# Stage one's value projection by seven block products, opened with the products that need no input sums

## The chip, the cores and the metric

The kernel runs on one core of a Trainium2 chip, as one program. Its time is the device time in microseconds of one execution. A core has TensorE (PE, matrix products, with its weight loads listed apart as PEld), VectorE (DVE), ScalarE (ACT), GpSimd (POOL) and SyncE (SP), whose queue issues nearly all of this kernel's DMA transfers. All of them run at the same time and wait for one another through semaphores. Smaller is better.

## The reference, cut to what matters

One layer with neighbourhood attention over a grid of 32 rows of 64 tokens, 16 heads of 64 columns:

```python
h = rmsnorm(x, g)                          # x: 2048 x 1024
proj = h @ w_in                            # 1024 x 4096: q, k, v, gate
q, k, v, gate = split(proj, 4)
o = neighbourhood_attention(q, k, v, rpb)  # softmax over 8 x 16 neighbours
x = x + (o * silu(gate)) @ w_out
return rmsnorm(x, norm_f)
```

All inputs and outputs are float32. The change is in how a part of `v` (the values) is computed.

## The kernel before

**Numbers.** Every float32 operand of a large product is split into a high part `h` and a low part `l`. A product is then three matmuls: high by high, high by low, low by high. One matmul takes a 128x128 block as weights and streams 512 columns.

**Stages.** `stage_one` projects the first 1024 tokens (the column blocks c = 0 and 1 of 512 tokens), `stage_two` most of the rest, then the attention runs with the remaining projections between its steps, and `rows_by_seven` computes the output rows. Each engine works through its instructions in the order in which the program issues them; a few DMA stores are put off by a number of matmuls (`store`, counted by `due`).

**Seven products.** q, k and the gate of stage one are computed in twelve units (`us`: k0 to k3, then q0, g0, q1, g1 and so on). A unit is a product of 2x2 blocks, and `seven_products` makes it from seven block products rather than eight (Winograd's form). The table `uses` names the weight block and the input block of each product P: product 1 takes A11 and B11, product 2 takes A12 and B21, product 3 S4 and B22, product 4 A22 and T4, products 5, 6 and 7 the sums S1, S2, S3 and T1, T2, T3. S1 to S4 are sums of weight blocks (`sum_`, on VectorE), T1 to T4 sums of the normalised-gain input blocks B11, B12, B21, B22. Products 1 and 2 need no sum. One block product is four k by three matmuls, twelve in all. Products 1 and 2 share a PSUM bank, so do 6, 7 and 4, and so do 5 and 3: each is added onto what the bank holds, after VectorE or ScalarE has read it.

- `form(n, P)` makes the high part of a weight block on ScalarE and the low part on VectorE (lines L420 and L421).
- `keep(n)` copies product 1 out (L446, ScalarE); `add` (L451), `out_` (L456 and a multiply on GpSimd, L458) and `evac` (L351) read the other products on VectorE.
- `give` finishes a result and has it stored.
- `ahead(i)` asks for the next weights, makes the casts of the coming products and the sums of the next unit.

**Values of stage one.** They are computed without block sums: `values_of` (L562) takes two halves u of the columns, eight row tiles t of 128 tokens and eight k, three matmuls each. `load_v0` and `split_v` (L542, L545) bring and split the weights, `evac_v` (L394) scales a tile by the token's inverse norm and stores it to `vd`. All of these products stand at the start of the kernel, ahead of the first unit. Meanwhile the inputs are loaded and split (L523, L524), the token rows are loaded and squared on ScalarE (`square`, L207), `stats(c)` computes the inverse norms of a column block on VectorE (L212 to L216), `diagonal(c)` and `spread_rstd(c)` spread them over the partitions by a small matmul (L223 to L236), the input sums are made on VectorE (L786 to L800) and T1 to T4 are split (L520, L521).

**Buffers.** Tiles come from pools with a fixed number of buffers: `ev` has eight (temporaries, evicted values, some rows), `raw` six (loaded weights), `wp` eight (split weights), `sp`, `qp`, `kp`, `ep` two each, `xp` eight; PSUM has eight banks. A tile waits until the last user of the buffer that it takes over is done, a DMA store included.

**Values of stage two.** They are already computed by seven products (`values_product`, L948), from the sums of the weight blocks. Stage one makes these sums (`value_rows`, `value_sum`, `value_split`) and stores them to `vsd` and `vsp`; stage two loads them back (`load_s`, `split_s`).

Of the kernel before, what the change touches and what calls it, by code (L numbers as in the profile page):

```python
# [1 line left out]

# [8 lines left out]
F32 = mybir.dt.float32  # L11
# [10 lines left out]
NK = D // 128  # L22
# [54 lines left out]
def build(ctx, tc, x, xr, xt, wg, bias, w_out, n0, nf, out):  # L77
# [9 lines left out]
    vsp = {f: dram.tile([4, 2, 128, 512], F32, name=f"vsp{f}") for f in ("S2", "S3")}  # L87
    wod = {f: dram.tile([128, 4, 2, 512], F32, name=f"wod{f}") for f in ("T1", "T2", "T3", "T4")}
# [316 lines left out]
    def seven_products(us, c0, X1, also):  # L405
# [5 lines left out]
        def load_w(n, f):  # L411
            A[n, f] = raw([128, 512], F32, "raw")
# [30 lines left out]
        def keep(n):  # L443
            kind = us[n][0]
            U[n, 1] = ep([128, 512], F32, "p1")
            nc.scalar.activation(lay(kind, U[n, 1]), of(kind, B[n, 1]), AF.Copy)  # L446
# [27 lines left out]

        def run():
            then = []
            for i, (n, P) in enumerate(seq):
                product(n, P)
                kind, j = us[n]
                now, then = then, []  # L480
                if P == 1:
                    keep(n)
                elif P == 6:
                    add(n, "2", 6)
                elif P == 2:
                    if c0 == 0:
                        evac(kind, 2 * j, c0, B[n, 2], then)
                    else:
                        then.append(lambda kind=kind, j=j, p=B[n, 2]: give(kind, 2 * j, c0, p, True))
                elif P == 7:  # L490
                    add(n, "3", 7)
                elif P == 5:
                    out_(n, 1, c0 + 1, 5, U[n, "3"], then)
                elif P == 4:
                    out_(n, 1, c0, 4, U[n, 1], then)
                elif P == 3:
                    out_(n, 0, c0 + 1, 3, U[n, "2"], then)
# [7 lines left out]
        return ahead, run  # L505
# [46 lines left out]
    def values_of(X1, u, ts, ks):  # L552
        for t in ts:
            if ks[0] == 0:
                ps[t] = bank(512, "pv")
        for k in ks:
            x = X1["B%d%d" % (k // 4 + 1, ts[0] // 4 % 2 + 1)][k % 4]
            h, l = W[u, k // 2][0][:, k % 2], W[u, k // 2][1][:, k % 2]
            for m, (a, b) in enumerate(((x[0], h), (x[0], l), (x[1], h))):
                for t in ts:  # L560
                    o = slice(t % 4 * 128, t % 4 * 128 + 128)
                    nc.tensor.matmul(ps[t], a[:, o], b, start=k == 0 and m == 0, stop=k == NK - 1 and m == 2)  # L562
                    due(1)

# [7 lines left out]

    def stage_one():
        us = [("k", j) for j in range(4)] + [(k, j) for j in range(4) for k in "qg"]
        X1 = {f: [(xs([128, 512], F32R, "h"), xs([128, 512], F32R, "l")) for _ in range(4)]
              for f in ("B12", "B11", "B21", "B22")}
# [3 lines left out]
        land["x12"] = [kp([128, 960], F32, "land")[:, :512] for _ in range(2)] + [xp([128, 512], F32, "land") for _ in range(2)]  # L580
        sixth = sixths()
        land["x21"] = [spot[:, k] for k in range(3)] + [lp([128, 512], F32, "land")]
        slots = [(mp, 512)] * 8 + [(sp, 512)] * 2 + sixth[:2] + [(vh, 512)] * 4
        slots += sixth[2:] + [(mp, 512)] * 2 + [(qp, 512)] * 2

        def load(f, k):
            load_x(0, f, k, land[f][k])

        def split(f, t, k, scale=None):
            if f == "T1":  # L590
                X1.setdefault(f, []).append((xs([128, 512], F32R, "h"), xs([128, 512], F32R, "l")))
            elif f[0] == "T":
                X1.setdefault(f, []).append((place_of(slots.pop(0)), place_of(slots.pop(0))))
            split_to(*X1[f][k], t, scale and gain(scale, k))
# [3 lines left out]
        def load_rows(*hs):  # L598
            for t, j in hs:
                rows_in[t, j] = mp([128, 512], F32, "row")  # L600
                nc.sync.dma_start(rows_in[t, j], xr[t * 128:t * 128 + 128, 512 * j:512 * j + 512])

        def square_rows(*hs):
            for t, j in hs:
                square(t, j, rows_in.pop((t, j)))
# [26 lines left out]
        def also(n, i):  # L632
            m = n + len(us) - 1
            if m < 8:
                if m % 2 == 0 and i == 0:
                    value_rows(m // 2)
                if m % 2 == 0 and i in (3, 4, 5, 6):
                    value_sum(m // 2, ("S1", "S3", "S2", "S4")[i - 3])
                if m % 2 == 1 and i in (1, 3):
                    value_split(m // 2, "S3" if i == 1 else "S2")  # L640
            if (m, i) == (4, 0):
                reorder_rstd(0)
                reorder_rstd(1)
            if m < 8 and i == 2:
                more_rows[m] = xp([128, 512], F32, "row"), xp([128, 512], F32, "row")
                for j in range(2):
                    nc.sync.dma_start(more_rows[m][j], xr[(8 + m) * 128:(9 + m) * 128, 512 * j:512 * j + 512])
            if m < 8 and i == 6:
                for j, t in enumerate(more_rows.pop(m)):
                    square(8 + m, j, t)  # L650
                if m in (3, 7):
                    stats(2 + m // 4)
            if (n, i) == (-3, 1):
                diagonal(2)
            if (n, i) == (-3, 3):
                spread_rstd(2)
            if (n, i) == (-3, 5):
                spot2 = mkp([128, 3, 512], F32, "spot")
                L2["x11"] = [spot2[:, k] for k in range(3)] + [lp([128, 512], F32, "land")]
                for k in range(4):  # L660
                    load_x(2, "x11", k, L2["x11"][k])
            if (n, i) == (-2, 2):
                L2["x21"] = [xp([128, 512], F32, "land") for _ in range(4)]
                for k in range(4):
                    load_x(2, "x21", k, L2["x21"][k])
            if (n, i) in norms:
                f, k = norms[n, i]
                normed(f, 2, k, L2[f][k])
            if (n, i) == (-3, 4):
                diagonal(3)  # L670
            if n == 0:
                if i == 0:
                    for a, b in ((0, 0), (1, 0), (0, 1)):
                        load_v0(0, a, b)
                    X2["B11"] = [(xs([128, 512], F32R, "h"), xs([128, 512], F32R, "l")) for _ in range(4)]
                    for k in (0, 1):
                        split_to(*X2["B11"][k], L2["x11"][k], None)
                elif i == 1:
                    for a, b in ((1, 1), (0, 2), (1, 2)):
                        load_v0(0, a, b)  # L680
                    for k in (2, 3):
                        split_to(*X2["B11"][k], L2["x11"][k], None)
                    split_v(0, 0, 0)
                    split_v(0, 1, 0)
                elif i == 2:
                    X2["B21"] = [(xs([128, 512], F32R, "h"), xs([128, 512], F32R, "l")) for _ in range(4)]
                    split_v(0, 0, 1)
                elif i == 3:
                    split_v(0, 1, 1)
                    L2["x12"] = [vh([128, 512], F32, "land") for _ in range(4)]  # L690
                    for k in range(4):
                        load_x(2, "x12", k, L2["x12"][k])
                    for a in range(2):
                        load_v0(0, a, 3)
                elif i in (4, 5):
                    for k in (0, 1) if i == 4 else (2, 3):
                        split_to(*X2["B21"][k], L2["x21"][k], None)
                    if i == 5:
                        split_v(0, 0, 2)
                        split_v(0, 1, 2)  # L700

        norms = {(-2, 3): ("x11", 0), (-2, 5): ("x11", 1), (-1, 0): ("x11", 2), (-1, 1): ("x11", 3),
                 (-1, 3): ("x21", 0), (-1, 4): ("x21", 1), (-1, 5): ("x21", 2), (-1, 6): ("x21", 3)}
        ahead, run = seven_products(us, 0, X1, also)

        parts_ = slice(0, 256), slice(256, 512)
# [8 lines left out]
        for b in (1, 2, 3):  # L715
            for j in range(2):
                for a in range(2):
                    if b == 1:
                        load_v0(0, a, b, cols=parts_[j])
# [1011 lines left out]
```

## Time and profile before

| | before |
|---|---|
| timed runs | 1019.26, 1022.46, 1022.52 us; median 1022.46 |
| the profiled execution | 1019.49 us, span 1017.7 us |
| TensorE busy, mean granted clock | 1007.7 us, 0.998 |
| VectorE busy | 776.2 us |
| ScalarE busy | 506.8 us |
| moved by DMA | 218 MB, 214 GB/s |
| stage one's values (L562) | 384 matmuls, from 4.5 to 93.6 us of the span |
| stage one's units (L438) | from there to about 322 us |

The page gives busy times, shares and counts of each engine, and the span in 40 slices. In an answer by windows a row has, for each engine, the busy time and the number of instructions, then the granted clock of TensorE (1.00 is full speed), the share of the DMA engines and GB/s. In an answer in order of time a row has the start, the length, the engine, the line, the operation and what stood idle before it, with its releaser in brackets; matmuls overlap in the pipeline, so their pace is read from start to start. A row of waits names who waited for whom, the sum, the number of times and the longest.

### The profile page before, as it was taken

How to read it: one execution, taken by the hardware profiler on the slowest of the kernel's cores; microseconds unless marked ns; L12 is line 12 of the kernel's file. 1: busy time of each engine (PE TensorE's matmuls, PEld its weight loads, DVE VectorE, ACT ScalarE, POOL GpSimd, SP SyncE). 2: the span in 40 equal slices, each digit the busy share in tenths (PEclk: the TensorE clock that was granted, in tenths of full speed). 3: DMA queues.
4: the chain of work that ended last, by engine and by line, in shares of the span. 5: the costliest groups of instructions: out<-in, count | busy, mean ns of one | idle time of the engine just before them, and what ended most of it. 6: DMA issues, size and time to landing. Idle time of an engine off the chain costs nothing. (4 is left out here: it accounts for less than half of the span.)

```text
span 1017.7 us, 19608 instructions
## 1 busy us (share of the span) xinstructions
PE 1007.7 (99%) x6952; PEld 805.9 (79%) x6952; DVE 776.2 (76%) x1712; ACT 506.8 (50%) x1241; POOL 175.0 (17%) x244
## 2 busy tenths in 40 slices
PE   9999999999999999999999999999999999999997
PEld 7888888888888888888888777777777777778876
DVE  6385878899798876766776577688898888787876
ACT  7645323444435442343433456577677657563343
POOL 0000132232132000000000033233242322320100
PEclk9999999999999999999999999999999999999999
DMA  9634667575537836657465787879888589799553
GB/s 317 241 104 121 187 210 225 169 227 186 167 102 218 258 125 186 200 181 219 168 196 191 224 261 242 261 245 292 266 257 274 184 242 305 210 346 365 140 160 104
DMA packets 142602, 218.23 MB, mean 214 GB/s; under 512 B 13032, under 2 KB 60392, under 8 KB 142504
## 3 DMA queue, kind: packets, MB, share of 16 engines
q1 hardware_dynamic: 140632, 213.96, 66.6%
q0 software_dynamic: 1440, 2.62, 1.7%
q8 instruction: 55, 0.90, 0.3%
q14 instruction: 43, 0.35, 0.1%
q10 hardware_dynamic: 432, 0.40, 0.1%
HBM read 151.92 MB, written 65.01 MB: 213 GB/s over the span
## 5 line engine op out<-in xcount | busy, mean ns | idle before, releaser
L438 PE MATMUL pp<-h,f 128*128 128x512 f32 x672 | 217.5, 389 | 0.0
L1166 POOL TENSOR_SCALAR x<-x,st 128x360 f32<-128x360 f32 (+5 forms) x192 | 106.5, 572 | 473.3 <-DVE st L1159 473.0
L1154 ACT ACTIVATE x<-x,st 128x360 f32<-128x360 f32 (+5 forms) x256 | 134.2, 525 | 26.4 <-DVE st L1148 26.4
L438 PEld LDWEIGHTS pp<-h,f 128*128 128x128 f32 x672 | 126.1, 188 | 26.2
L438 PE MATMUL pp<-t,f 128*128 128x512 f32 x558 | 141.7, 389 | 0.1
L438 PE MATMUL pp<-l,f 128*128 128x512 f32 x336 | 130.7, 389 | 0.0
L438 PEld LDWEIGHTS pp<-t,f 128*128 128x128 f32 x558 | 104.6, 188 | 22.3 <-DVE u L451 0.6
L458 POOL TENSOR_TENSOR tmp<-tmp,rb 128x512 f32<-128x512 f32 x36 | 59.0, 1641 | 268.1 <-DVE tmp L456 231.0
L1148 DVE CUSTOM_DVE_ANT_0 x<-s,em 128x360 f32<-128x360 f32 (+5 forms) x256 | 102.5, 454 | 2.2 <-PE s L1139 1.4
L421 DVE TENSOR_TENSOR f<-raw,f 128x512 fp32r<-128x512 f32 x105 | 75.1, 716 | 29.5 <-ACT f L420 29.3
L1213 PEld LDWEIGHTS o<-pta,vt 120*64 120x64 f32 (+2 forms) x1024 | 68.8, 137 | 22.6 <-DVE st L1148 15.2
L1213 PE MATMUL o<-pta,vt 120*64 120x192 f32 (+5 forms) x1024 | 83.4, 316 | 0.3 <-issue 0.3
L1183 DVE COPY pta<-ph 120x512 f32<-120x512 f32 (+5 forms) x96 | 56.0, 638 | 32.7 <-PE ph L1194 32.5
L1139 PE MATMUL s<-kt,q 64*64 64x360 f32 (+5 forms) x1024 | 78.7, 420 | 1.2 <-DVE y L1289 1.0
L420 ACT ACTIVATE f<-raw 128x512 fp32r<-128x512 f32 x105 | 63.6, 622 | 31.3 <-DMA raw<-in_wg_dram 13.5
L1185 ACT ACTIVATE pta<-ph 120x512 f32<-120x512 f32 (+5 forms) x96 | 46.8, 558 | 62.4 <-PE ph L1194 62.3
L438 PEld LDWEIGHTS pp<-l,f 128*128 128x128 f32 x336 | 63.1, 188 | 13.1
L1139 PEld LDWEIGHTS s<-kt,q 64*64 64x64 f32 x1024 | 41.5, 131 | 23.1 <-ACT pta L1185 6.1
L438 PE MATMUL pp<-sixths,f 128*128 128x512 f32 x198 | 54.6, 389 | 0.0
L420 ACT ACTIVATE f<-s 128x512 fp32r<-128x512 f32 x42 | 26.2, 625 | 53.5 <-DVE s L427 49.8
L1499 PE MATMUL py<-woh,f 128*128 128x512 f32 x160 | 50.9, 390 | 0.9 <-DVE y L1289 0.9
L1194 PEld LDWEIGHTS ph<-ident,x 64*120 64x120 f32 (+2 forms) x1408 | 42.5, 128 | 11.3 <-issue 9.5
(209 smaller groups left out, 1911.4 us busy)
## 6 DMA issues: line engine op xcount, KB each, us to landing
raw<-in_wg_dram SPq DMA_DIRECT2D x120, 256.0 KB, 5.0
row<-in_xr_dram SPq DMA_DIRECT2D x32, 256.0 KB, 5.3
vd<-v SPq DMA_DIRECT2D x32, 256.0 KB, 2.7
sgd<-sg SPq DMA_DIRECT2D x32, 256.0 KB, 3.5
q<-qd SPq DMA_DIRECT2D x32, 256.0 KB, 5.4
sgt<-sgd SPq DMA_DIRECT2D x32, 256.0 KB, 7.2
ogd<-og SPq DMA_DIRECT2D x32, 256.0 KB, 2.7
kt<-kd SPq DMA_DIRECT2D x16, 480.0 KB, 6.2
```

Source lines behind the costliest of these rows:

```text
L420: nc.scalar.activation(t[:, 0], src, AF.Copy)
L421: nc.vector.tensor_tensor(t[:, 1], src, t[:, 0].bitcast(F32), OP.subtract)
L438: nc.tensor.matmul(B[n, P], t[:, int(m == 2), c], x[k][int(m == 1)], start=P in (1, 6, 5) and k == 0 and m == 0, stop=k == 3 and m == 2, s ...
L458: nc.gpsimd.tensor_tensor(tmp, tmp, rb[c], OP.mult)
L1139: nc.tensor.matmul(pst[s][h * 64:h * 64 + 64], qt[a, g * 64:g * 64 + 64], kt[a, :r1 - r0, c0:c0 + 8 * WIDE[C]].rearrange("p r (s c) -> p s ...
L1148: nc.vector.tensor_tensor_reduce(X[i, C][s], pst[s], EM[p, ROW_TYPE[T]][C > 0][s], -1.0, 1e38, OP.add, OP.min, st[:, o:o + 1])
L1154: nc.scalar.activation(X[i, C][s], X[i, C][s], AF.Exp, bias=st[:, o:o + 1], scale=-1.0, accum_out=st[:, 4 + o:5 + o])
L1166: nc.gpsimd.tensor_scalar(X[i, C][s], X[i, C][s], st[:, o:o + 1], 1.0, op0=OP.mult, op1=OP.mult)
L1183: nc.vector.tensor_copy(o, i_)
L1185: nc.scalar.activation(o, i_, AF.Copy)
L1213: nc.tensor.matmul(o[s * 64:s * 64 + 64, g0 * 64:g1 * 64], vt[:k, strip, s * 64:s * 64 + 64], t[:k, n * 64:(n + g1 - g0) * 64], start=stri ...
L1499: nc.tensor.matmul(B[m, P], t[:, a, c], b, start=P in (1, 6, 5) and k == 0 and i == 0, stop=k == 3 and i == 2, skip_group_check=True)
```

## The change

The values of stage one become a 2x2 block product of their own, made by the same seven products as everything else, and the order of stage one is written anew:

- The kernel opens with the values' product 1 (`first_values`, k = 0 to 3, four row tiles). ScalarE copies it out, and it is stored to a new buffer `vu1` in device memory. Two units' product 1 follow (steps 0 and 1), then the values' product 2 onto the same banks (k = 4 to 7), then the other first products of the units 0 to 5: `seq` holds for these six units all products 1 and 2 first (steps 0 to 11).
- The input sums are made and split between these steps. Then three pairs of units run interleaved (steps 12 to 41), ten products each, and the units 6 to 11 in the usual order (steps 42 to 83). `step` issues one product, then what is to follow it; `on` puts other work behind a step by its number.
- The weights A11 and A12 of the units 2 to 5 are loaded twice.
- The values' remaining five products (P = 6, 7, 5, 4, 3, four row tiles each: `late_value`) come last, with the sums S1 to S4 that stage one has made for stage two anyway; `load_u1` brings `vu1` back. `give_v` adds on VectorE and scales on GpSimd.
- The normalising and splitting of stage two's first inputs, which stood in the last units of stage one, moves beside these late products.

Stage two takes `load_s`, `split_s`, `w_of` and the product's loop from common functions, and splits its value weights of k 4 and 5 at its own first step.

```diff
@@ seven_products
+        parts = SimpleNamespace(load=load_w, form=form, sum=sum_, product=product, keep=keep, after=after, B=B)
+        return ahead, run, parts
...
-    def values_of(X1, u, ts, ks):
...
+    def part_of_values(p, X, P, i):
+        o = slice(i * 128, i * 128 + 128)
+        for k in range(4):
+            x, w = X[uses[P][1]][k], [a[:, k % 2] for a in W[w_of[P][k // 2]]]
+            for m, (a, b) in enumerate(((x[0], w[0]), (x[0], w[1]), (x[1], w[0]))):
+                nc.tensor.matmul(p, a[:, o], b, start=P in (1, 6, 5) and k == 0 and m == 0, stop=k == 3 and m == 2,
+                                 skip_group_check=True)
+                due(1)
...
+        E, C = 6, 42
+        seq = [(n, P) for ns in (range(4), range(4, 6)) for P in (1, 2) for n in ns]
+        for a in (0, 2, 4):
+            seq += [(a + i, P) for i, P in ((0, 6), (1, 6), (0, 7), (0, 5), (1, 7), (0, 4), (1, 5), (0, 3), (1, 4), (1, 3))]
+        seq += [(n, P) for n in range(E, len(us)) for P in order7]
...
+        def step(i):
+            n, P = seq[i]
+            seven.product(n, P)
+            now, then[:] = then[:], []
+            if i >= 2 * E:
+                seven.after(n, P, then)
+            elif P == 1:
+                seven.keep(n, kp([128, 960], F32, "p1")[:, :512] if n > 3 else accs[n - 2] if n > 1 else None)
+            for f in now:
+                f()
+            for f, a in todo.pop(i, ()):
+                f(*a)
+
+        def first_values(k, ts=(0, 1, 2, 3)):
+            x = X1["B%d1" % (k // 4 + 1)][k % 4]
+            h, l = W[0, k // 2][0][:, k % 2], W[0, k // 2][1][:, k % 2]
+            for m, (a, b) in enumerate(((x[0], h), (x[0], l), (x[1], h))):
+                for t in ts:
+                    if k == 0 and m == 0:
+                        ps[t] = bank(512, "pv")
+                    nc.tensor.matmul(ps[t], a[:, t * 128:t * 128 + 128], b, start=k == 0 and m == 0, stop=k % 4 == 3 and m == 2,
+                                     skip_group_check=True)
+                    due(1)
...
+        for t in range(4):
+            u = ev([128, 512], F32, "u1v")
+            nc.scalar.activation(u, ps[t], AF.Copy)
+            nc.sync.dma_start(vu1[t], u)
...
+        for k in range(4, 8):
+            first_values(k)
+            sums1(k - 4)
+            split("B22", "x22", (k - 4,), "x22")
+            sums(k - 4)
+        step(2)
+        square_rows(0, range(4))
+        forms(5)
+        step(3)
+        square_rows(0, range(4, 8))
         stats(0)
+        forms(7)
+        for n in (4, 5):
+            seven.load(n, "A12", sp)
+        for f in ("A21", "A22"):
+            seven.load(0, f)
+        load_rows(1, range(4), ev)
+        step(4)
         for t in range(4):
             evac_v(0, t, ps[t])
+        split("T1", "x12", (0, 1), "x11")
+        step(5)
+        split("T1", "x12", (2, 3), "x11")
+        diagonal(0)
+        forms(9)
+        for f in ("A21", "A22"):
+            seven.load(1, f)
+        step(6)
+        split("T2", "x11", (0, 1))
+        step(7)
+        spread_rstd(0)
+        split("T2", "x11", (2, 3))
+        forms(11)
+        square_rows(1, range(4))
+        load_rows(1, range(4, 8), ev)
+        step(8)
...
+        step(11)
+        square_rows(1, range(4, 8))
+        stats(1)
+        seven.sum(1, "S3")
+        first_out(3)
+        forms(14)
...
+        on(12, diagonal, 1)
+        on(12, t4, 0, 1)
+        on(13, t4, 2, 3)
+        on(14, spread_rstd, 1)
...
+        for j in range(4):
+            on(C + 9 * j, value_rows, j)
...
+        on(N - 6, diagonal, 2)
+        on(N - 4, spread_rstd, 2)
+        on(N - 5, load_s, "S2", 0, 1)
+        on(N - 4, load_s, "S2", 2, 3)
+        on(N - 4, load_u1)
+        on(N - 3, load_next, "x11")
+        on(N - 3, load_s, "S1", 0, 1, 2, 3)
+        on(N - 2, load_s, "S3", 0, 1)
+        on(N - 2, diagonal, 3)
+        for i in range(2 * E, N):
+            step(i)
+            forms(i + (3 if i < C - 4 else 4 if i < C else 5 if i < C + 3 else 6))
...
+        def late_value(P, i):
+            if P in (6, 5):
+                VB[P, i] = bank(512, "pv")
+                for Q in {6: (7, 4), 5: (3,)}[P]:
+                    VB[Q, i] = VB[P, i]
+            p = VB[P, i]
+            part_of_values(p, X1, P, i)
+            if P in (6, 7):
+                U = U2 if P == 6 else U3
+                U[i] = (ev if P == 6 else xp)([128, 512], F32, "u%d" % P)
+                nc.vector.tensor_tensor(U[i], p, U1[i], OP.add)
+            else:
+                give_v(int(P != 3), i if P == 4 else 4 + i, p, {5: U3, 4: U1, 3: U2}[P][i])
...
+        for P in (6, 7, 5, 4, 3):
+            for i in range(4):
+                late_value(P, i)
```

More of the change, by code (lines that the diff above doesn't have):

```diff
@@ L1 @@
 from contextlib import ExitStack
+from types import SimpleNamespace
 import numpy as np
@@ L478, in run @@
                 product(n, P)
-                kind, j = us[n]
                 now, then = then, []
[L481 to L497, printed above, removed]
+                after(n, P, then)
                 for f in now:
@@ L808, in t1 @@
-        def t1(*ks):
-            return lambda: [split("T1", land["x12"][k], k, "x11") for k in ks]
-        v = lambda t: lambda: evac_v(1, t, ps[t])
-        tile_v(4, some("T2", "x11", 0, 1, 2, 3))
-        tile_v(5, v(4), t4, slot(-9), some("T3", "x22", 0, 1))
-        tile_v(6, v(5), some("T3", "x22", 2, 3), slot(-8, -7))
-        tile_v(7, v(6), lambda: diagonal(0), some("T4", "x21", 0), slot(-6))
-        tile_v(0, v(7), lambda: spread_rstd(0), some("T4", "x21", 1), lambda: diagonal(1))
@@ new lines, in stage_one @@
+        diagonal(0)
[11 more added lines that the diff above has]
+        step(8)
+        seven.sum(0, "S1")
+        seven.sum(0, "S2")
+        first_out(0)
+        forms(12)
+        step(9)
+        seven.sum(1, "S1")
+        seven.sum(1, "S2")
```

464 lines of the change are left out of this document (239 added, 225 removed).

## The prediction

> **What bounds the kernel now.** I read the page first (the engines' busy time, the slices), then the waits of TensorE alone, then windows of ten microseconds through the opening and one per unit of stage one, and last the order of time inside the opening.
>
> ```profile
> span 1017.7 us, 19608 instructions
> PE 1007.7 (99%) x6952; PEld 805.9 (79%) x6952; DVE 776.2 (76%) x1712; ACT 506.8 (50%) x1241; POOL 175.0 (17%) x244
> PE zp L133 <- DVE z L130: 1.2, 1, 1.2
> PE s L1139 <- DVE y L1289: 1.0, 1, 1.0
> 50.00:60.00 10.00, 10.00 (x46) 8.29 (x45) 9.89 (x16) 7.06 (x13) 0.00 (x0) 1.00 0.47 119
> 60.00:70.00 10.00, 10.00 (x46) 8.29 (x45) 9.83 (x19) 4.77 (x9) 0.00 (x0) 1.00 0.49 136
> ```
>
> TensorE is busy for 1007.7 of 1017.7 us; its two longest waits are 1.2 us (the start) and 1.0 us (the output rows). Stage one has next to no idle on it, at full clock. So each product taken away is worth its whole pace, and each new wait of TensorE costs its whole length. The same windows show VectorE at 9.9 of 10 us from 50 to 70 us: it then makes the input sums and their splits while the plain value products cover it.
>
> The profiled execution took 1019.49 us, 1.8 more than its span. The three timed runs are 1019.26, 1022.46 and 1022.52, so their median lies 3 us above it, and runs of the changed kernel may scatter alike. I sum against 1019.5, and 0.3% (3.1 us) is what a measurement of this kernel can tell from no change.
>
> **What is removed.** One product is twelve 128x512 matmuls.
>
> ```profile
> 13.91 1.07 PE L562 MATMUL pv<-wh,h 128*128 128x512 f32 x4
> 16.63 1.07 PE L562 MATMUL pv<-wh,h 128*128 128x512 f32 x4
> ```
>
> These rows open two successive k of the values, twelve matmuls apart: 2.72 us, 0.227 us a matmul. Before: 8 row tiles x 2 halves x 8 k x 3 = 384 matmuls. After: 7 products x 4 tiles x 4 k x 3 = 336. The difference of 48 is four products, **-10.9 us**. The Trainium skill (Perfetto Trace Analysis, "Identifying the Most-Contended Engine") holds matmul busy time for a bad measure and takes the weight loads' share instead. By that share, 79%, the four products would be worth 8.6 us; but the pace above runs without a gap, so the row decides.
>
> **What the opening loses.** Before, all 32 value products (87 us) stood ahead of the first product that needs an input sum. Now eight value products and twelve unit products do, and the squares, statistics, T1 to T4 and the units' first casts share that shorter time. I call t=0 the end of step 2: 16.63 plus seven products, 35.7 us. From there TensorE has five products, 13.6 us, to the spread of rb[0], where before it was never short. The prices of the work on the other engines:
>
> ```profile
> 19.78 0.63 ACT L207 ACTIVATE row<-row 128x512 f32<-128x512 f32 x1
> 20.42 0.63 ACT L207 ACTIVATE row<-row 128x512 f32<-128x512 f32 x1
> 28.75 0.16 DVE L212 TENSOR_TENSOR m<-ss 128x4 f32<-128x4 f32 x1 [0.40 <-ACT row L207]
> 31.33 0.17 DVE L216 TENSOR_SCALAR rth<-rt 128x4 f32<-128x4 f32 x1
> 31.59 2.42 ACT L394 ACTIVATE v<-pv,rth 128x512 f32<-128x512 f32 x4 [2.88 <-DVE rth L216]
> 48.45 3.23 ACT L542 ACTIVATE wh<-raw 128x512 fp32r<-128x512 f32 x6
> 83.62 1.94 ACT L523 ACTIVATE h<-land,g 128x512 fp32r<-128x512 f32 x3
> 60.93 2.49 DVE L521 TENSOR_TENSOR t<-land,t 128x512 fp32r<-128x512 f32 x4
> 17.35 3.40 DVE L524 SCALAR_TENSOR_TENSOR l<-land,g,h 128x512 fp32r<-128x512 f32 x5
> 96.78 0.60 ACT L446 ACTIVATE p<-pp 128x512 f32<-128x512 f32 x1 [2.03 <-PE pp L438]
> 69.00 0.86 DVE L223 TENSOR_SCALAR dg<-ident,rt 128x128 f32<-128x128 f32 x4
> 70.56 0.69 DVE L227 TENSOR_TENSOR dgl<-dg,dgh 128x512 fp32r<-128x512 f32 x1 [0.70 <-ACT dgh L226]
> ```
>
> From start to start: a square 0.64; the statistics 2.75 in all; a value evicted 0.58; a cast 0.52, with a scale 0.61; a VectorE subtraction 0.60, with a scale 0.66; a product copied 0.60; the diagonal and its split 2.25 in one chain. A reader starts 0.2 us after the last matmul:
>
> ```profile
> 104.74 0.39 PE L438 MATMUL pp<-h,f 128*128 128x512 f32 x1
> 104.94 0.69 DVE L451 TENSOR_TENSOR u<-pp,p 128x512 f32<-128x512 f32 x1 [0.83 <-PE pp L438]
> ```
>
> The waits, in order (ScalarE and VectorE work in program order):
>
> A, step 4. ScalarE: 0.2, keep(2) 0.55, four squares 2.6, the cast of F(0,2) 0.6 = 3.9; VectorE's low half 0.7, used two matmuls (0.45) later: step 4 can start at 4.15. TensorE holds only step 3 (2.7) as cover: **1.4**.
>
> B, step 6. ScalarE goes on: cast to 4.35, keep(3) 4.9, four squares 7.5; 0.2 and stats(0) 2.75 on VectorE 10.4; behind it the low half of F(2,2) 11.1, less 0.45. TensorE ends step 5 at 9.6: **1.0**. Who waits behind stats(0): forms(7) on VectorE and the four evictions on ScalarE.
>
> C, the spread after step 7. Evictions 10.6 to 12.9, four scaled T1 casts to 15.4, VectorE behind them to 16.1, then 2.25 for the diagonal: 18.3; TensorE is there at 16.1, a wait of 2.1 if the buffers are free. They are not: ev has eight, and four rows of the next column block and the four evicted values hold all of them. diagonal(0) takes three, from values whose stores must have landed. Those stores stand on SP behind eight loads, of which the first, the A12 of unit 4 into sp, waits for F(2,2) at 11.1.
>
> ```profile
> 95.75 1.88 SPq L616 DMA_DIRECT2D vs<-in_wg_dram  x4
> DMA to landing us min/median/max: 2.2/2.6/5.5
> 10.00:20.00 10.00, 10.00 (x45) 8.28 (x45) 9.39 (x16) 9.57 (x17) 0.00 (x0) 1.00 1.02 372
> ```
>
> Eight issues at 0.47 put the first store at 14.9; landing takes 2.2 to 5.5 (the values' own stores), and 9 x 262 KB at 372 GB/s are 6.3 us behind 11.1, so about 18.6; the third buffer 1.4 later. The dgl is then done near 21: **4.7** (2.1 if stores land at once, 6.5 if later).
>
> D, step 10 (4,2). After dgh at 20.3 ScalarE has eight casts 4.2, rb[0] 0.55, four squares 2.6 and keep(4) 0.6, to 28.2; steps 8 and 9 end at 26.7: **1.5**.
>
> E, step 14 (0,7), which adds onto the bank that VectorE must read first. ScalarE from 28.2: ten casts and copies 5.2, four squares 2.6, some 1.7 of waiting for S2 of unit 1 and for an eviction by VectorE, 37.7; stats(1) 2.95, a sum, an eviction, a cast's half and the add 2.5: 43.1. TensorE is there at 39.1: **3.8** (2.3 without the waiting).
>
> F, steps 15 and 16. Ahead of F(0,5) VectorE has diagonal(1) with its wait, two T4 sums and splits, 5.4, less 0.45, against 3.2 on TensorE: 1.8; ahead of F(1,7) 4.0 against 2.7: 1.2. **3.0** (1.5 if E is shorter). After that VectorE has 17 operations of 0.6 in a pair's last five products and catches up.
>
> Sum of the waits: 15.4, between 9 and 18.
>
> **What else moves.** Eight more loads of 256 KB (A11 and A12 of units 2 to 5 twice, four stored P1 and their return as well) cost nothing on TensorE except C: the DMA share is 0.47 in the 50 to 60 us row above. The values' own sums (24 operations) come every nine products instead of every fourteen:
>
> ```profile
> 227.00:246.00 19.00, 19.00 (x86) 15.72 (x85) 17.43 (x23) 9.04 (x18) 5.63 (x4) 1.00 0.59 187
> 265.20:284.30 19.10, 19.10 (x86) 15.82 (x85) 14.69 (x22) 8.41 (x15) 4.73 (x4) 1.00 0.68 214
> 284.30:303.30 19.00, 19.00 (x86) 15.73 (x85) 18.09 (x25) 7.00 (x12) 4.65 (x3) 1.00 0.23 69
> 207.10 1.62 POOL L458 TENSOR_TENSOR tmp<-tmp,rb 128x512 f32<-128x512 f32 x1 [1.29 <-ACT f L420]
> 207.48 1.78 DVE L421 TENSOR_TENSOR f<-s,f 128x512 fp32r<-128x512 f32 x1
> ```
>
> A unit without them holds VectorE for 14.7 of 19 us; six operations per nine products add 2.8 at 0.6 each: 17.5. The unit at 284 us ran 18.1 with no TensorE idle, so I take 0; a VectorE operation under a POOL one took 1.78 instead of 0.69, and if the added ones met all three POOL operations of a unit (3 x 1.1), it would need 20.8 us, 1.7 too many: 9 us over the 36 products, 6 if they meet two of three. The end of stage one (load_u1 waits on SP for out_(11,4), two products; S2, S1, x11 and S3 queue behind it) has 10.9 us of P=6 products as cover: 0, up to 2 if S3 lands late. Normalising and splitting stage two's inputs now lies under 54 us of value products, where VectorE has 52 operations of 0.6 to 0.7 (8 normalisings, 24 splits, 20 reads of products), 34 us: 0. The POOL scalings of the values are off TensorE's path: 0. One price is left, the clock:
>
> ```profile
> 4.53 1.22 PE L562 MATMUL pv<-wh,h 128*128 128x512 f32 x2
> 7.09 0.62 PE L562 MATMUL pv<-wh,h 128*128 128x512 f32 x2
> 1010.00:1014.00 4.00, 1.70 (x8) 1.09 (x6) 3.28 (x10) 2.94 (x10) 0.00 (x0) 0.97 0.32 123
> 1014.00:1017.70 3.70, 0.00 (x0) 0.00 (x0) 0.15 (x1) 0.39 (x1) 0.00 (x0) 0.50 0.40 151
> ```
>
> TensorE's last matmul ends at 1011.7; a mean of 0.97 over the four microseconds puts the fall to 0.5 at 1013.8, 2.1 us later. At the start six matmuls took 2.56 us (4.53 to 7.09) instead of 1.36. So a wait beyond 2.1 us (C and E) may cost 1.2 more at its end. In E the slower products give VectorE the time that F asks for; I count it once: **+1.2**. The Trainium skill (TensorE: Matmul & The Clock Gate, "The HAM clock gate") has a free-running window of about 3.4 us; by it C and E would both count, 2.4, and the tail's 2.1 us agrees with a window that was partly over.
>
> Forecast: 1019.5 - 10.9 + 15.4 + 1.2 = **1025 us**.
>
> **Rivals.** (1) Faster: the waits are mostly covered. C falls to 2.1 because the stores land at once, E and F vanish because VectorE, no longer blocked at the diagonal, is ahead; 1.4 + 1.0 + 2.1 + 1.5 = 6.0 remain: 1019.5 - 10.9 + 6.0 = 1014.6. For it: VectorE is idle for some 4 us of C in my own chain, and TensorE never waited before. Against: A, B and D hang on ScalarE's order alone, and stats(1) stays behind eight squares. Turning point: waits under 7.8 us. Chance 0.25. (2) No change: the waits lie between 7.8 and 14, that is C near 2 with E whole: 1020. Chance 0.2. (3) Slower by VectorE's overload in units 6 to 11, beside the opening: one mechanism, the value sums meeting POOL's operations; it decides once a unit needs more than 19 us: 1025 + 6 = 1031. Chance 0.12. (4) Slower by the clock alone, each wait above 2.1 us resuming at half pace, with F not relieved: 1025 + 2.4 = 1027. It stands within my own case. Forecast's case (with 4): 0.43.
>
> **The numbers.** Slower by over 0.3%: 0.43 + 0.12 = 0.55; within 0.3%: 0.2; faster: 0.25. The low end 1012.5 takes in most of rival 1 (waits of 4 us), the high end 1032 rival 3; some 2 in 10 lie outside.
>
> **What would show it.** Right: between 35 and 90 us TensorE idles some 15 us, after "DVE dgl", "ACT p" and "DVE u"; VectorE waits at the diagonal for a store of vd; the granted clock dips below 1.00 in some of those windows; units 6 to 11 and the late values run without a gap; the value lines hold 336 matmuls. Wrong: TensorE's waits before 95 us sum to under 8 us (rival 1), or its windows after 100 us show idle (rival 3).

## The result, and the profile after

The changed kernel takes 1036.66 us (median of 4 runs, 1035.28 to 1038.27); the kernel before took 1020.87 beside it (1019.26 to 1022.52). The ratio is 1.0155, interval 1.0128 to 1.0182: slower, by 15.8 us where 5.5 were forecast. The profiled span grew by 17.3 us. The page of the changed kernel and the waits of its TensorE:

```profile
span 1035.0 us, 19617 instructions
PE 1005.0 (97%) x6904; PEld 798.6 (77%) x6904; DVE 783.7 (76%) x1732; ACT 500.4 (48%) x1233; POOL 201.5 (19%) x256
```

```profile
PE prb L234 <- ACT dgh L228: 4.6, 1, 4.6
PE pv L594 <- DMA wh<-vspS: 4.3, 2, 2.3
PE pp L440 <- DVE u L453: 4.0, 4, 1.8
PE pp L440 <- ACT f L422: 3.0, 3, 1.3
PE pp L440 <- DVE f L423: 1.5, 1, 1.5
```

The 48 matmuls are gone (6952 to 6904), but TensorE's busy time fell by only 2.7 us, in part because some of what is left runs at half clock. Before, the longest wait was 1.2 us; now there are some 18 us of new ones. Nearly all of the loss is made in stage one: the first scores of the attention start 16.5 us later than before, and the last wait ahead of them that is new ends at 297 us. The first row is from the order of time of the kernel before, the second of the changed one:

```profile
573.84 0.38 PE L1139 MATMUL s<-kt,q 64*64 64x176 f32 x4
```

```profile
590.33 0.75 PE L1267 MATMUL s<-kt,q 64*64 64x176 f32 x12
```

The windows of the changed kernel (columns: window and its length, busy time and count of PE, PEld, DVE, ACT and POOL, granted clock, DMA share, GB/s) show where:

```profile
50.00:60.00 10.00, 5.43 (x22) 3.85 (x21) 4.05 (x10) 2.89 (x6) 0.00 (x0) 0.97 0.89 280
42.00:46.00 4.00, 3.43 (x9) 2.71 (x10) 2.92 (x13) 2.82 (x8) 0.00 (x0) 0.57 0.00 0
58.00:62.00 4.00, 2.69 (x6) 1.85 (x7) 2.95 (x7) 3.37 (x7) 0.00 (x0) 0.67 0.30 85
200.00:210.00 10.00, 10.00 (x46) 8.29 (x45) 10.00 (x14) 5.81 (x12) 2.64 (x2) 1.00 0.63 197
280.00:290.00 10.00, 9.36 (x40) 7.08 (x39) 7.59 (x12) 4.79 (x10) 1.62 (x1) 1.00 0.99 320
290.00:300.00 10.00, 5.35 (x17) 3.64 (x18) 3.06 (x6) 1.58 (x4) 0.00 (x0) 0.91 1.04 373
298.00:302.00 4.00, 4.00 (x12) 3.12 (x11) 1.89 (x3) 0.00 (x0) 0.00 (x0) 0.57 0.82 294
```

There are two wounds. One is the opening, which was foreseen. The other, at 290 to 300 us, lies in the late values and was forecast at nothing: TensorE is busy for 5.35 of 10 us while the DMA engines are full. In between, VectorE at 10.00 of 10 us (200 to 210) costs TensorE nothing. TensorE's order of time, at the waits and the matmul ahead of each:

```profile
38.73 0.39 PE L440 MATMUL pp<-h,f 128*128 128x512 f32 x1
40.38 0.50 PE L440 MATMUL pp<-h,f 128*128 128x512 f32 x1 [1.26 <-ACT f L422]
40.72 0.40 PE L440 MATMUL pp<-l,f 128*128 128x512 f32 x1
42.57 1.22 PE L440 MATMUL pp<-h,f 128*128 128x512 f32 x2 [1.46 <-DVE f L423]
...
54.35 0.39 PE L440 MATMUL pp<-h,f 128*128 128x512 f32 x1
59.31 0.78 PE L234 MATMUL prb<-dgh,onesr 128*128 128x512 f32 x1 [4.57 <-ACT dgh L228]
...
79.94 0.93 PE L440 MATMUL pp<-t,f 128*128 128x512 f32 x3 [1.77 <-DVE u L453]
...
289.20 0.39 PE L594 MATMUL pv<-wh,t 128*128 128x512 f32 x1
291.92 0.47 PE L594 MATMUL pv<-wh,t 128*128 128x512 f32 x1 [2.33 <-DMA wh<-vspS]
...
296.41 0.47 PE L594 MATMUL pv<-wh,sixths 128*128 128x512 f32 x1 [1.93 <-DMA wh<-vspS]
```

What a wait costs is read from start to start, less the pace of 0.227 us: 38.73 to 40.38 costs 1.42, 54.35 to 59.31 costs 4.73, 289.20 to 291.92 costs 2.49. Summed up to the first scores in this way, with the matmuls that ran slowly, TensorE loses 29.4 us; the kernel before lost 2.15. 29.4 - 2.15 - 10.9 = 16.4, against the 16.5 us above. Such a sum closes by construction, since every interval between two starts is in it: it says where the time lies, and not what made it.

The releasers behind it, in the order of time of VectorE and then of SP's queue:

```profile
41.84 1.28 DVE L423 TENSOR_TENSOR f<-raw,f 128x512 fp32r<-128x512 f32 x2
...
57.36 0.88 DVE L225 TENSOR_SCALAR dg<-ident,rt 128x128 f32<-128x128 f32 x4 [4.90 <-DMA vd<-v]
```

```profile
272.39 5.95 SPq L904 DMA_DIRECT2D u<-vu  x4
...
278.86 1.64 SPq L519 DMA_DIRECT2D spot<-in_xt_dram  x3
...
281.04 3.92 SPq L579 DMA_DIRECT2D raw<-vsdS  x4
285.22 0.54 SPq L576 DMA_DIRECT2D wh<-vspS  x1
...
291.27 0.60 SPq L576 DMA_DIRECT2D wl<-vspS  x1
```

At 57.36 the diagonal has waited 4.90 us until stored values gave back its buffers. At the end, S3's first half is asked for at 285.22, behind u (its four requests take 5.95 us, most of it a wait), x11 (from 278.86) and S1 (from 281.04). The late products run in the order P = 6, 7, 5, that is S2, S3, S1: SP asks for S1 first though S3 is needed first. The matmul that needs the first part of S3 starts at 291.92, 6.7 us after that part was asked for.

### The profile page after: what moved, and what is told of

The parts are those of the page before. It is cut to its first block, busy times and chain, and to the rows that moved or that the text cites. A ratio compares the mean times of both kernels' runs of the same rounds, so it can differ in the third digit from the quotient of the medians.

```text
span 1035.0 us, 19617 instructions
## 1 busy us (share of the span) xinstructions
PE 1005.0 (97%) x6904; PEld 798.6 (77%) x6904; DVE 783.7 (76%) x1732; ACT 500.4 (48%) x1233; POOL 201.5 (19%) x256
## 5 line engine op out<-in xcount | busy, mean ns | idle before, releaser
L440 PE MATMUL pp<-h,f 128*128 128x512 f32 x576 | 187.5, 393 | 2.7 <-DVE f L423 1.5
L440 PE MATMUL pp<-t,f 128*128 128x512 f32 x702 | 173.2, 390 | 5.8 <-DVE u L453 4.0
L440 PEld LDWEIGHTS pp<-t,f 128*128 128x128 f32 x702 | 131.2, 188 | 36.1 <-issue 3.5
L440 PEld LDWEIGHTS pp<-h,f 128*128 128x128 f32 x576 | 109.4, 190 | 26.4 <-DVE f L423 1.9
L440 PE MATMUL pp<-l,f 128*128 128x512 f32 x288 | 113.0, 392 | 0.0
L423 DVE TENSOR_TENSOR f<-raw,f 128x512 fp32r<-128x512 f32 x105 | 79.4, 761 | 23.0 <-ACT f L422 22.8
L440 PEld LDWEIGHTS pp<-l,f 128*128 128x128 f32 x288 | 54.6, 190 | 11.5
L594 PE MATMUL pv<-wh,t 128*128 128x512 f32 x176 | 56.8, 392 | 2.3 <-DMA wh<-vspS 2.3
```

Source lines behind the costliest of these rows:

```text
L423: nc.vector.tensor_tensor(t[:, 1], src, t[:, 0].bitcast(F32), OP.subtract)
L440: nc.tensor.matmul(B[n, P], t[:, int(m == 2), c], x[k][int(m == 1)], start=P in (1, 6, 5) and k == 0 and m == 0, stop=k == 3 and m == 2, s ...
L594: nc.tensor.matmul(p, a[:, o], b, start=P in (1, 6, 5) and k == 0 and m == 0, stop=k == 3 and m == 2, skip_group_check=True)
```

## The experiments

Each is compared with the changed kernel unless it says otherwise, and its ratio is against the kernel before, which ran beside it (1019.18 us median of 8 runs for the first four, 1019.04 of 9 for the others). The changed kernel was not run again beside them, and the kernel before took 1020.87 us beside it, so a difference between two times below is uncertain by some 1.8 us. Against the kernel before that ran beside each, the changed kernel is 15.8 us slower, experiment 1 10.0 and experiment 2 11.0.

**1. The order of SP's queue at the end of stage one.** S3 ahead of u, x11 and S1:

```diff
-        on(N - 4, load_u1)
-        on(N - 3, load_next, "x11")
-        on(N - 3, load_s, "S1", 0, 1, 2, 3)
         on(N - 2, load_s, "S3", 0, 1)
+        on(N - 2, load_u1)
         on(N - 2, diagonal, 3)
+        on(N - 1, load_next, "x11")
...
-            (6, 0): [(load_s, "S3", 2, 3), (load_next, "x21"), (spread_rstd, 3)],
+            (6, 0): [(load_s, "S3", 2, 3), (load_s, "S1", 0, 1, 2, 3), (load_next, "x21"), (spread_rstd, 3)],
```

> Only the order of SP's issues at the end of stage one changes: S3 is asked for ahead of the returning P1 and of x11, and S1 behind S3. Theory L (the late values wait for S3 because S1, x11 and the returning P1 stand ahead of it on a saturated DMA): the waits of 2.3, 0.7 and 1.9 us of line L594 after 288 us go, and with them the 3.4 us at half clock behind them (1.7 us); 7.6 us faster than the changed kernel, about 1029 us. Rival V (the late part is bound by VectorE's reads and by the amount of DMA, whatever its order): the waits move to x11, S1 or U1, within 2 us of 1036.7.

Measured: 1029.17 us, ratio 1.0092 (1.0072 to 1.0112), 7.5 us less (5.8 by the differences to the kernel before). No wait on vspS is left, and the window of the late values is whole:

```profile
290.00:300.00 10.00, 10.00 (x45) 8.26 (x44) 6.69 (x12) 5.14 (x10) 0.00 (x0) 1.00 0.82 303
```

The same bytes still move, at 303 GB/s. So it was the order in which they were asked for, and this alone is over a third of the loss. By the account of stage one the gain was 9.0 us there (7.4 left of 16.4), of which 7.7 in the late values and 0.9 at the kernel's start, which the edit does not touch. The span is 11.0 us longer than that of the kernel before, so 3.6 were lost behind stage one: among them a wait of 1.4 us in the output rows, and a fall of the clock told in the last section.

**2. The diagonal's buffers.** The rows that fill `ev` go to another pool:

```diff
-        load_rows(1, range(4), ev)
+        load_rows(1, range(4), xp)
```

> The four row tiles of the second column block are loaded into xp instead of ev, one word. Theory C (diagonal(0) waits for a buffer of ev, that is for the store of an evicted value): VectorE's idle of 4.9 us before diagonal(0) goes, the wait of TensorE before the spread falls from 4.6 to about 2 us, no half clock follows; the time falls by 2.6 to 4.5 us, to about 1033 us. Rival D (VectorE and ScalarE are short of time in any case): the waits of lines L440 at 80 to 90 us grow by what the spread's wait loses; no change.

Measured: 1030.21 us, ratio 1.0117 (1.0089 to 1.0145), 6.5 us less, which is more than expected (4.8 by the differences to the kernel before). The waits of TensorE, first of all the spread's:

```profile
PE pv L594 <- DMA wh<-vspS: 3.4, 2, 3.0
...
PE pp L440 <- ACT p L448: 0.9, 1, 0.9
PE prb L234 <- ACT dgh L228: 0.7, 1, 0.7
```

The spread's wait falls from 4.6 to 0.7; 0.9 of it comes back two products later. So the buffers held by stores, not the diagonal's own work, made that wait. From start to start, the spread and the product behind it lose 5.1 us less than in the changed kernel, 1.7 of it the stretch at half clock, and 1.1 is lost anew two products later: 4.0, within what was expected. What the first scores gain beyond that (8.0 in all) lies elsewhere: 2.0 in the late values and 0.8 at the start, where the edit changes nothing, and 1.5 at step 4, behind which the clock did not fall, though the waits there are as long as before (1.23 + 1.46 us). It fell at step 14 instead, where the slow matmuls took the place of the wait ahead of step 15.

**3. Matmuls put into the waits to keep the clock up** (6 ahead of step 4, 14 ahead of the spread, 8 ahead of the late P = 7; their results are used by nothing):

```diff
+        def dummies(n):
+            p = bank(512, "dm")
+            for _ in range(n):
+                nc.tensor.matmul(p, X1["B11"][0][0][:, :128], X1["B11"][0][0], start=True, stop=True)
```

> Matmuls into an unread bank are added: 6 before step 4 (1.4 us), 14 before the spread of rb[0] (3.2 us), 8 before the late P=7 (1.8 us). All stand in the waits of 3.0, 4.9 and 2.5 us. Theory K (an idle stretch halves the granted clock for 3.4 us, which costs 1.7 us each time): the first two half-clock stretches go, perhaps the third too, and the time falls by 3.4 to 5 us, to about 1032 us, although TensorE has 6.3 us more work. Rival S (the half-clock stretches lie in time that the other engines need anyway): 1036 to 1038 us, the waits behind them grow by as much.

Measured: 1041.69 us, ratio 1.0215 (1.0198 to 1.0231). It is 5 us slower than the changed kernel, outside both expectations, and decides neither: the first bank that they took still belonged to a value that ScalarE had not read, which made a wait of its own.

```profile
PE dm L739 <- ACT v L396: 9.4, 1, 9.4
```

**4. The 48 matmuls alone.** The kernel before with the third matmul left out in six tiles of half 1 of the values, which are then less exact:

```diff
-            for m, (a, b) in enumerate(((x[0], h), (x[0], l), (x[1], h))):
+            short = u == 1 and ts[0] in (4, 5, 6, 7, 0, 1)
+            for m, (a, b) in enumerate(((x[0], h), (x[0], l), (x[1], h))[:2 if short else 3]):
```

> The kernel before, in which 48 matmuls of the values are left out (the product of low inputs and high weights in six tiles of the second half of the columns), so that part of the computation is missing. It measures the first term of the sum by itself. Theory P (TensorE's pace bounds stage one): 48 x 0.227 = 10.9 us faster than before, about 1010 us. Rival W (the weight loads' share, 79%, is what counts, or the other engines fill the opening): 8.6 us or less.

Measured: 1013.45 us, ratio 0.9946 (0.9926 to 0.9965). The median fell by 5.7 us and the span of the profiled execution by 7.3 (1017.7 to 1010.4), not by 10.9, and there is a new wait:

```profile
PE prb L232 <- ACT dgh L226: 2.2, 1, 2.2
...
PE prb L233 <- DVE dgl L227: 0.5, 2, 0.2
```

These 2.7 us and the restarts behind them are about 3 of the missing 3.6; 0.6 stays unexplained. By the number rival W came out, and by its second half, in which the other engines set the pace of the opening. Its first half, the weight loads' share, is not borne out, since the trace has the new wait in its place. So the pace holds once the wait is added, and even in the old order the work beside the values had no more than about 8 us to spare.

**5. Both repairs, and the casts of step 4 earlier.** Experiments 1 and 2 together, with `forms(5)` ahead of the input sums and `forms(7)` ahead of the squares of rows 4 to 7:

```diff
+            if k == 6:
+                forms(5)
...
-        forms(5)
         step(3)
+        forms(7)
         square_rows(0, range(4, 8))
         stats(0)
-        forms(7)
```

> The later order of SP's issues and the rows in xp together, and the casts of F(0,2), F(1,2) ahead of VectorE's last two input sums and of F(2,2), F(3,2) ahead of four squares and stats(0). Theory I (the waits are separate, each with its own cause): the gains add up, 7.5 + 6.5 + 3 for the wait before step 4: about 1019.5 us, level with the kernel before. Rival Q (in the opening ScalarE and VectorE are short of time, and what is taken from one wait reappears in the next): the casts' 3 us reappear at the spread and at (0,7), about 1022.5 us.

Measured: 1023.79 us, ratio 1.0045 (1.0031 to 1.006). This is near rival Q and not theory I: the gains did not add up. The wait at step 4 is gone, and the spread's is back although its buffers are free:

```profile
PE prb L234 <- ACT dgh L228: 3.8, 1, 3.8
```

In VectorE's order of time the diagonal now stands behind no store (no wait in brackets); it comes late because the statistics, ScalarE's evictions and casts and VectorE's low halves of T1 stand ahead of it (orders of time of ScalarE and VectorE):

```profile
47.32 2.42 ACT L396 ACTIVATE v<-pv,rth 128x512 f32<-128x512 f32 x4 [2.90 <-DVE rth L218]
...
50.38 2.74 DVE L530 SCALAR_TENSOR_TENSOR t<-land,g,t 128x512 fp32r<-128x512 f32 x4 [3.16 <-ACT t L529]
53.03 0.87 DVE L225 TENSOR_SCALAR dg<-ident,rt 128x128 f32<-128x128 f32 x4
```

The clock is at 0.67 in the window from 52 to 56 us and at 0.50 from 56 to 60. What step 4 no longer waits for, the spread does: the work ahead of it on ScalarE and VectorE is the same, and TensorE arrives sooner. Rival Q calls this a shortage of time, but neither engine is busy throughout: from 44 us on ScalarE stands idle for 2.90 us until the statistics are done, VectorE then for 3.16 us until ScalarE's evictions and first cast are. It is a chain that passes from one engine to the other, with the diagonal as its last link.

**6. The opening in another order.** Experiment 5 with `diagonal(0)` right behind `stats(0)`, `forms(9)` ahead of the evictions, the squares of the second column block behind step 8 and behind step 11's casts, and its statistics, diagonal, T4 and spread one to two steps later:

```diff
         stats(0)
+        diagonal(0)
...
+        forms(9)
         for t in range(4):
             evac_v(0, t, ps[t])
...
-        diagonal(0)
-        forms(9)
...
+        step(8)
         square_rows(1, range(4))
...
-        square_rows(1, range(4, 8))
-        stats(1)
...
-        forms(14)
+        forms(15)
+        square_rows(1, range(4, 8))
...
+        on(12, stats, 1)
         on(12, diagonal, 1)
-        on(12, t4, 0, 1)
-        on(13, t4, 2, 3)
+        on(13, t4, 0, 1)
+        on(14, t4, 2, 3)
```

> e5 with the opening put in another order: diagonal(0) right behind stats(0), the casts of units 4 and 5 ahead of the evictions, keep(4) ahead of four squares, the squares and stats of the second column block behind the add of (0,6), T4 one step later. The work is the same. Theory Q (the opening has too little time for ScalarE and VectorE, whatever the order): some 8 us of waits remain between 35 and 95 us, 1018 us, at best 3 us faster than the kernel before and not 10.9. Rival O (the order alone makes the waits): they fall under 3 us in all and the time to 1011 us.

Measured: 1022.7 us, ratio 1.0035 (1.0022 to 1.0048): the best order tried, still slower than the kernel before and than either theory had it. With the diagonal right behind the statistics the spread waits 1.0 us and no longer 3.8, now for an eviction. The waits between 35 and 95 us sum to 5.6 us, between the 8 of theory Q and the 3 of rival O; they have scattered:

```profile
PE pp L440 <- DVE u L453: 2.3, 3, 1.0
PE pp L440 <- ACT p L448: 2.0, 1, 2.0
...
PE prb L234 <- ACT dgh L228: 1.0, 1, 1.0
PE pp L440 <- ACT f L422: 1.0, 1, 1.0
...
PE prb L234 <- ACT v L396: 1.0, 1, 1.0
```

The last row is the spread of rb[0]. Two of the three waits in the first row (1.03 and 1.01 us) lie in the later pairs, past the opening.

**7. Matmuls into the spread's wait alone** (14, as in experiment 3, in a bank that is free):

```diff
         step(7)
+        dummies(14)
         spread_rstd(0)
```

> Fourteen matmuls (3.2 us) into an unread bank ahead of the spread of rb[0], in its wait of 4.9 us; the changed kernel otherwise. This time the bank is free when they are issued. Theory K (the idle stretch halves the granted clock for 3.4 us and costs 1.7 us): no half clock behind the spread, 1.7 us faster than the changed kernel, 1035 us. Rival S (the slow stretch lies in time that ScalarE and VectorE need anyway): no change within 1 us, and steps 10 to 16 wait longer.

Measured: 1035.93 us, ratio 1.0166 (1.0151 to 1.0181): no gain. The spread's wait shrinks to 0.7 us and no half clock follows it (granted clock, last but two, 1.00 from 57 to 61 us). But it falls further on, and for longer at the late values, and 0.9 us is waited two products later. In this execution the waits at step 4, ahead of the matmuls put in, were 1.6 us longer as well (2.82 + 1.46), so the trace does not say by itself what the filled wait was worth; the times say no more than 0.7 us.

```profile
57.00:61.00 4.00, 3.08 (x13) 2.00 (x12) 2.44 (x7) 2.23 (x5) 0.00 (x0) 1.00 0.67 200
80.00:84.00 4.00, 3.91 (x11) 3.16 (x12) 3.22 (x8) 1.74 (x3) 0.00 (x0) 0.60 0.28 92
...
294.00:298.00 4.00, 3.45 (x8) 2.07 (x7) 0.00 (x0) 0.00 (x0) 0.00 (x0) 0.50 1.07 374
```

**8. Without the squares.** The 16 squares of ScalarE in the opening are replaced by constants; the rows are still loaded:

```diff
-            for h in hs:
-                t, j = 4 * c + h // 2, h % 2
-                square(t, j, rows_in.pop((t, j)))
+            if c not in rows:
+                rows[c] = tiny.tile([128, 8], F32, name="ss")
+                nc.gpsimd.memset(rows[c], 512.0)
```

> The changed kernel with the sixteen squares of the first two column blocks left out (the sums of squares are set to a constant, so that part of the computation is missing; the rows are still loaded). Theory A (10.4 us of squares on ScalarE stand ahead of the casts, of stats and of keep(4)): the wait at step 4 loses ScalarE's 1.4 us, the waits before the spread, at (4,2) and at (0,7) shrink, no half clock follows: 5 to 8 us faster, 1029 to 1032 us. Rival B (VectorE's sums and splits alone set these waits): under 2 us faster.

Measured: 1033.43 us, ratio 1.0132 (1.0112 to 1.0153): 1.4 us less by the differences to the kernel before, 3.2 by the times, for some 10 us of ScalarE's work (16 squares at 0.64). Both are under theory A's 5 to 8. The wait at step 4 goes over to VectorE, which makes the input sums, and is no shorter (3.6 us against 1.26 + 1.46):

```profile
PE pp L440 <- DVE f L423: 3.6, 1, 3.6
...
PE prb L234 <- ACT dgh L228: 0.7, 1, 0.7
```

So VectorE's input sums alone set the wait at step 4. The spread's wait is gone, but not by ScalarE's time: a row that nothing squares gives its buffer of `ev` back when its load has landed, and the diagonal now waits for "DMA row<-in_xr_dram", for 2.30 us, where it waited 4.90 for a store. From start to start the spread loses 5.2 us less than in the changed kernel, as in experiment 2, and steps 4 and 14 lose 0.8 and 1.5 more. The squares' own time is not shown to bind anything.

## Why the prediction was right or wrong

The direction was right, and so was the mechanism in the opening; the time lay above the range, because of terms that the sum had at nothing or too small. Against 15.4 us of waits and 1.2 of clock the trace has 22.1 of waits and slow restarts and 5.1 of clock, by the account from start to start:

| term | predicted | measured |
|---|---|---|
| 48 matmuls | -10.9 | -10.9 |
| start | 0 | 0.6 |
| A, step 4 | 1.4 | 3.0 |
| B, step 6 | 1.0 | 0 |
| C, the spread | 4.7 | 4.7 |
| D, step 10 | 1.5 | 0 |
| E, step 14 | 3.8 | 1.9 |
| F, steps 15 and 16 | 3.0 | 3.0 |
| later pairs | 0 | 2.7 |
| end of stage one, waits | 0 (up to 2) | 5.9, and 0.3 at a spread ahead of it |
| clock | 1.2 | 5.1 |
| sum | 5.7 | 16.3 |

**The removal.** Right: the counts agree, and experiment 4 finds the pace, but for 0.6 us, once its new wait is taken off.

**The opening.** The six waits A to F sum to 12.6 us against 15.4; that this is near is partly luck, since A was too small and B, D and E too large. C came out in cause: the diagonal stood 4.90 us behind "DMA vd<-v", and experiment 2 removed it by buffers alone. Its size came out by luck as well, for TensorE reached the spread 18.3 us after the end of step 2 instead of 16.1, and the diagonal's high part was there as much later. A was mis-sized: I had the input sums out of VectorE's way, but VectorE was at them until 41.84, so ScalarE's cast was only the first half of the wait (1.26) and VectorE's low half the second (1.46). B and D did not appear, and E was half its forecast. My reading is that each wait, and each slow stretch behind it, gives the engines the time that the next one asks for, and that I had chained them with too little of that; no run shows it by itself.

**The step that failed: the end of stage one**, "0, up to 2 if S3 lands late". I had named the queue (u, then S2, S1, x11, S3) and not worked it out. u holds it for 5.95 us; x11 and S1 then go ahead, and with DMA full (shares of 0.99 and 1.04) S3 lands so late that the late P = 7 waits 5.9 us and runs on at half clock for 1.7: 7.6, and experiment 1, which moves only those requests, took 7.7 off the late values. The row for 284 to 303 us, in which the DMA share was 0.23 before, was read for VectorE alone; the late values' loads, which the change puts there, fill it.

**The clock.** "I count it once" at 1.2 failed too. There were three stretches, behind A, C and S3, of 3.4 us each and 1.7 us lost in each (42 to 46 us: 0.57 of 4 us is 3.44 us at half). The 2.1 us taken from the kernel's end was no threshold: the two waits at step 4 were 1.26 and 1.46 us. By the Trainium skill (TensorE: Matmul & The Clock Gate, "The HAM clock gate") the window is about 3.4 us and free-running; the length agrees with these rows. The sum drawn from it, 2.4 for C and E, does not: E had no fall, A and S3 did.

**The later pairs.** VectorE was to catch up behind F. TensorE is idle again for 0.92 us at 111.86, 1.01 at 140.36 and 0.25 at 170.78. The first two stand at the place of E in the second and the third pair, without squares or statistics ahead of them, and VectorE's order of time shows what holds up the read of the bank:

```profile
108.73 0.68 DVE L429 TENSOR_TENSOR raw<-raw 128x512 f32<-128x512 f32 x1
110.19 0.92 DVE L423 TENSOR_TENSOR f<-raw,f 128x512 fp32r<-128x512 f32 x1 [0.78 <-ACT f L422]
111.04 0.68 DVE L453 TENSOR_TENSOR u<-pp,acc 128x512 f32<-128x512 f32 x1
```

VectorE makes a sum, waits 0.78 us for ScalarE's cast of it, makes the low half and only then reads product 6. This is the order of work in a pair, and not a backlog from the opening: with the opening changed, in experiments 2, 5 and 6, the two waits are 0.92 to 1.03 us long all the same. No experiment moved that read ahead.

**The rivals.** Rival 1 (covered waits) fell: the waits from 35 to 90 us exceed its turning point of 7.8. Of rival 2 (waits between 7.8 and 14) the sum came true, 12.6, and its form did not: C was 4.7 and not near 2, and E half. Rival 3 (VectorE's overload in units 6 to 11) fell: VectorE is full from 200 to 210 us and TensorE runs 46 matmuls there at full clock; the 0.25 us at 170.78 is TensorE's only wait ahead of the spread at the end of these units. Of rival 4, more stretches at half clock than one came true, at C and at places that it did not name. What I took as a sign of rightness, that the late values run without a gap, was the sign that failed.

**What is settled.** Experiments 1 and 2 show two causes by removing them, the queue's order at the end of stage one and the diagonal's buffers. Experiments 5 and 6 show that the opening's other waits move with the order of work; they do not tell whether ScalarE and VectorE have too little time there, for in experiment 5 both stand idle inside the chain to the diagonal. The later pairs' waits are in every version of the changed kernel. In experiment 6 the first scores start 2.4 us later than in the kernel before; the later pairs' two waits cost 2.4 there and the one stretch at half clock 1.7. Whether a better order exists stays open; none tried beats the kernel before.

## What to carry to other kernels

When work is taken from the engine that covers others, price the covered work anew: here four products saved 10.9 us and uncovered more. An engine's program order can hold up a read that frees a bank: look for it where the same wait comes back at the same step. Where DMA is full, write down the queue in order with each request's start and the time that its data is needed; data asked for early that is needed late delays what is needed now. A pool shared by a computation and by tiles waiting to be stored ties the computation to the landing of the stores, and one changed pool here brought 4 us at the place itself.

## What the runs showed of the hardware

Stretches at half clock came in 3.4 us or some multiple of it, and the length of the wait did not decide whether one came. Within an execution they lie on a grid: by the traces' record of the granted clock they began at 42.29, 59.36 and 298.29 us in the changed kernel, which is 5 and 70 times 3.413 us apart, and at 42.27, 76.40, 288.03 and 840.99 us in experiment 8, which is 10, 62 and 162 times that. So where a wait falls on the grid may bear on it, beside its length. The same wait of 1.01 us ahead of the same scores left the clock alone in the changed kernel and was followed by a fall in experiment 1; the orders of time, changed kernel first:

```profile
844.56 3.40 PE L1267 MATMUL s<-kt,q 64*64 64x192 f32 x32 [1.01 <-DVE y L1417]
```

```profile
835.60 4.69 PE L1266 MATMUL s<-kt,q 64*64 64x192 f32 x32 [1.01 <-DVE y L1416]
838.00:842.00 4.00, 4.00 (x39) 2.50 (x33) 2.54 (x13) 3.53 (x14) 1.44 (x4) 0.63 0.86 255
```

The same 32 matmuls took 4.69 us instead of 3.40. A cause was not isolated; ahead of the wait both orders of time have the same matmuls at the same distances, and what differs is when the wait falls. So single runs of two versions can differ by 1.7 us for each such stretch without any difference in their work, and a version's gain of a few microseconds is to be read from the waits, with the clock beside them.
